# Two feature groups of the first projection side by side, turned blocks in 1 KB runs, and readers two ticks later

## The chip, the cores and the metric

The kernel runs on one core of a Trainium2 chip. The metric is device time in microseconds of one execution, the median of several. TensorE (PE) multiplies, VectorE (DVE) and ScalarE (ACT) do elementwise work, GpSimd (POOL) and SyncE (SP) here do little but issue transfers; ACT issues a few too.

## What is computed

Two decoder layers over 256 tokens of width 2048, float32 throughout. Layer 0 mixes with a gated spatial unit (A) and a gated recurrence (B), layer 1 with attention (C); each is followed by a gated feed-forward block with a causal convolution of width 3 over the tokens. Cut to what matters here:

```python
for l in range(DEPTH):                     # DEPTH = 2
    h = rms_norm(x, mix_norm[l])
    h = mixer_ab(h, ...) if l % 2 == 0 else mixer_c(h, ...)
    x = x + h
    h = rms_norm(x, ffn_norm[l])
    x = x + conv_ffn(h, ...)

def mixer_ab(h, w_in, ...):                # u, v, q, f, i, g = 6 x 1024 columns
    u, v, q, f, i, g = jnp.split(h @ w_in, cuts, axis=-1)
    v = rms_norm(gelu(v), v_gain)          # per head of 128
    y_a = gelu(u) * (causal(sp_w) @ v + sp_b)
    y_b = hgrn2(q, f, i, g, ...)
    return jnp.concatenate([y_a, y_b], axis=-1) @ w_out

def conv_ffn(h, w_up, conv_w, conv_b, w_down):
    z = h @ w_up                           # 2 x 5632 columns
    z = sum(conv_w[j] * zp[:, j:j + seq] for j in range(3)) + conv_b
    a, b = jnp.split(z, 2, axis=-1)
    return (silu(a) * b) @ w_down
```

## The kernel before

**Layout.** The residual stream `xT` lies feature-major: 16 tiles of 128 features by 256 tokens. A float32 product is made of three passes over operands split into a high and a low part (float32r): high by high, high by low, low by high. `weights` (L157) takes one tile of weights (128 x 1024, 512 KB): SP loads `w`, ACT copies it to `wh` (L176), DVE subtracts to get `wl` (L179). There are four `w` and three `wh` and `wl` buffers, and in the FFN two more of each for every other tile. Activations are split likewise by `split` (L279), into `a[k]`, 512 columns: high, then low; `Norm.feed_split` makes them from `xT[k]` and the norm's gain, `feed_square` adds up the squares, `finish` and `finish_tok` sum them over the partitions on PE (L360, L349) and take the reciprocal root.

**Projections.** `project_tok` and `project_four` make a token-major result of 512 features, two banks `ps[0]`, `ps[1]` of 128 tokens each, from eight tiles of weights (chunks of two k), twelve matmuls of 512 columns a chunk. `project` makes one head of 128 features, feature-major, from two tiles. PSUM has four `pm` banks for these and four `px` banks for small products.

**Ticks.** Each projection calls `tick()` once before each of its weight tiles. A tick advances up to `depth` generators of the `queue`, in which the elementwise work that follows a projection is written: one `yield` is one tick. `LAG = 4` is the number of ticks that a reader leaves after a turned block was sent off. The program's order is a wish: a compile-time scheduler draws the final order of every engine's instructions from it and from a model of when operands are ready, and each engine then runs its own list in order.

**Turned blocks.** `transposed` (L254) turns a token-major result of 128 x 1024 to feature-major: DVE transposes 32 x 32 blocks into `tmp` (L257, two instructions), then 16 transfers of 32 KB, SBUF to SBUF, alternately from SP and POOL, move block (a, b) to its place (L262). A transfer reads 32 partitions of 1 KB and writes four runs of 256 B in each. The result has four feature tiles of 256 tokens, each tile in one run. Readers: the residual adds in `add_four` (L385, after both `w_out`) and `add_y` (L911, after `w_down`), which then feed the next norm; the convolution `conv` in the FFN (L865 on ACT, L866 and L867 on DVE); `attend` for q and k (L713); `gate` for the attention output (L811, L812).

**First projection.** `project_tok(w_v[g], norm, feed=g == 0)` (L420) runs group 0 of v's columns and then group 1. While it runs group 0, x arrives: SP loads x pieces and weights in an order fixed by hand (`in_turn`, first nine weight tiles). The first eight k are loaded in halves of 256 KB (`SMALL = 8`, `single`). Group 1 uses the `a[k]` made for group 0. The squares of the norm are summed during group 1 by the generator `finish` (L410), three k a tick; the squares may not start before the seventh tile's `wh` (`deep["hold"]`), and ACT's six late loads of constants (L435) hang on the same. `finish` ends with the first group's Gelu; `drain()` runs what is left of it. After the stage come the norm of v per head (L452 to L463), the eight f heads (`project_norm(w_f[h])`) and, from the fourth tick on, the products `mix` (L470).

**FFN.** `up(j0)` projects four tiles of the first half (`za`), starts `gate`, then four of the second half (`zb`), and starts `fill`; both wait for the norm, turn their block with `empty` (L846), let LAG ticks go, and do one feature tile a tick. `room` gives one `tmp` and two `zt` buffers; the convolution has six rotating buffers. `down` multiplies hidden tiles as they come (`STEPS`); the last step has eight hidden tiles, so a quarter of the output takes four chunks, and each quarter goes through `add_y`.

Of the kernel before, what the change touches and what calls it, by code (L numbers as in the profile page):

```python
# [8 lines left out]
F32 = mybir.dt.float32  # L9
# [3 lines left out]
ALU = mybir.AluOpType  # L13
# [12 lines left out]
LAG = 4  # L26
# [5 lines left out]
SMALL = 8  # L32
# [19 lines left out]
def tile_trunk(ctx: ExitStack, tc: tile.TileContext, x, pp_d, cst_d, mlev_d, msk_d,  # L52
# [91 lines left out]
    def in_turn(r):  # L144
        if deep["turn"] > 9:
            return
        if deep["dma"] is not None:
            tc.add_manual_dep(r.ins, deep["dma"].ins.name, order, reason="queue order")
        deep["dma"] = r
# [7 lines left out]
    def weights(src, n, rows=None, single=None):  # L157
# [8 lines left out]
        parts = [slice(i, i + n // 2) for i in (0, n // 2)] if single else [slice(0, n)]  # L166
        for i, p in enumerate(parts):
            if single:
                fetch_x(single[1] + i)
            in_turn(nc.sync.dma_start(  # L170
                w[:, p] if rows is None else w.rearrange("p (m c) -> p m c", m=rows), src[:, p] if single else src))
        for i, p in enumerate(parts):
            if single:
                norm, k = single
                norm.feed_split(k + i, SC if k + i else V)
            deep["act"] = SC.activation(wh[:, p], w[:, p], AF.Copy)  # L176
            if deep["turn"] == 7:
                deep["hold"] = deep["act"]
            V.tensor_tensor(wl[:, p], w[:, p], wh[:, p].bitcast(F32), ALU.subtract)  # L179
        return wh, wl  # L180

# [26 lines left out]
    def project_tok(wsrc, norm, feed=False):  # L208
        ps = [pm.tile([P, 512], F32, tag="pm", name=nm("pm")) for _ in range(2)]
        k = 0  # L210
        for c in (2,) * 8:
            if feed and k >= SMALL:
                fetch_x(k)
                for i in range(c):
                    norm.feed_split(k + i)
            tick()
            wh, wl = weights(wsrc[:, k * 512:(k + c) * 512], c * 512, single=(norm, k) if feed and k < SMALL else None)
            if feed and k < SMALL:
                for i in range(c):
                    a = norm.a[k + i]  # L220
                    for j, (o, t) in enumerate(((0, wh), (S, wh), (0, wl))):
                        for T in range(2):
                            PE.matmul(ps[T], a[:, o + T * P:o + (T + 1) * P], t[:, i * 512:(i + 1) * 512],
                                      start=k + i + j == 0, stop=False)
                k += c
                continue
            for T in range(2):
                for i in range(c):
# [6 lines left out]
            k += c  # L235
# [18 lines left out]
    def transposed(src, tmp, dst, queues=(nc.sync, nc.gpsimd)):  # L254
# [5 lines left out]
        for a in range(4):  # L260
            for b in range(4):
                queues[(a + b) % len(queues)].dma_start(dst[BLK * b:BLK * (b + 1), :, a * n:(a + 1) * n],  # L262
                                  tmp[BLK * a:BLK * (a + 1), b * 4 * n:(b + 1) * 4 * n]
                                  .rearrange("p (m r) -> p m r", m=4))
# [110 lines left out]
    def add_four(q, ps, z, tmp, dst, nxt):  # L375
# [4 lines left out]
        def rest():  # L380
            for _ in range(LAG - (q == 3)):
                yield
            for i in range(4):
                m = 4 * q + i
                V.tensor_tensor(xT[m], xT[m], dst[:, i], ALU.add)  # L385
# [11 lines left out]
    def mixer_ab(norm):  # L397
# [12 lines left out]
        def finish():  # L410
            for k in range(KT):
                norm.feed_square(k)
                if k % 3 == 2:
                    yield
# [5 lines left out]
        for g in range(2):  # L420
            ps = project_tok(w_v[g], norm, feed=g == 0)
            v = hp.tile([P, 2, 512], F32, tag="tok", name=nm("gv"), bufs=2)
            gv.append(v)
            if g == 0:
                SC.activation(v[:, 0], ps[0], AF.Copy)
                SC.activation(v[:, 1], ps[1], AF.Copy)
                queue.append(finish())
# [229 lines left out]
        for q in range(4):  # L657
# [3 lines left out]
            dst = stage[:, q % 2].rearrange("p h c -> p (h c)").rearrange("p (m t) -> p m t", m=4)  # L661
# [399 lines left out]
```

## Time and profile before

| what | value |
|---|---|
| median of 3 runs | 2309.99 us (2309.86 to 2310.22) |
| the profiled execution | 2308.94 us |
| its span | 2306.8 us |
| granted PE clock | 1.0 |
| busy DVE, ACT, POOL | 68%, 56%, 14% |
| HBM read | 435.24 MB, 190 GB/s over the span |
| DMA packets under 512 B | 106400 of 462243 |
| first projection | 4.87 to 51.45 us |
| mixer C starts | 1112.4 us |

A line of the timeline gives start and duration in us, engine, line of the kernel, operation, the tile written and those read, the shape and how many were merged; in brackets, how long the engine had been idle and what ended that. A line of waits gives the waiting engine and line, what it waited for, the total in us, how often, and the longest. A line on one tile or source line gives the least, median and greatest duration in ns. A window's line gives its length, busy us and instruction count of PE, PE's weight loads, DVE, ACT and POOL, then the granted clock, the DMA engines' busy share and GB/s.

### The profile page before, as it was taken

The page shows a single profiled execution, that of the slowest core. Times are in us where ns is not written, and L with a number is a line of the kernel's source. Part 1 is how long each engine was busy: PE and PEld are TensorE (multiplying, and loading weights), DVE is VectorE, ACT ScalarE, POOL GpSimd, SP SyncE. Part 2 cuts the span into 40 slices and gives each one's busy share as a digit, 9 for nine tenths or more (in the row PEclk, how much of TensorE's full clock was granted, in tenths as well). Part 3 has the DMA queues.
Part 4 walks back from the last instruction along what each step waited for, and adds up shares of the span by engine and source line. Part 5 has one row for each costly group of instructions (what it writes and reads, how often), then busy time and mean ns, then how long its engine had stood idle before and what let it go on. Part 6 is the DMA issues. An engine that isn't in the chain of part 4 may idle for free. (4 is left out here: it accounts for less than half of the span.)

```text
span 2306.8 us, 31666 instructions
## 1 busy us (share of the span) xinstructions
PE 2298.1 (100%) x10608; PEld 1915.4 (83%) x10608; DVE 1575.4 (68%) x2407; ACT 1301.9 (56%) x1972; POOL 311.8 (14%) x579
## 2 busy tenths in 40 slices
PE   9999999999999999999999999999999999999999
PEld 7888888888888888888888888888888888888887
DVE  7778876776557656765866666666776476667666
ACT  7655665665555545654555555655665465455643
POOL 0000002122012002111111101121221022012102
PEclk9999999999999999999999999999999999999999
DMA  8655567877667767776666565777777677667765
GB/s 276 182 167 154 155 195 215 253 222 211 210 208 209 220 196 215 217 217 192 190 229 201 182 192 168 224 220 241 234 219 208 202 215 213 206 204 218 221 202 174
DMA packets 462243, 477.25 MB, mean 207 GB/s; under 512 B 106400, under 2 KB 424880, under 8 KB 461952
## 3 DMA queue, kind: packets, MB, share of 16 engines
q1 hardware_dynamic: 441840, 451.96, 63.6%
q0 software_dynamic: 18512, 20.93, 4.0%
q10 hardware_dynamic: 1728, 2.35, 0.3%
q8 instruction: 83, 1.36, 0.3%
q14 instruction: 80, 0.66, 0.1%
HBM read 435.24 MB, written 2.11 MB: 190 GB/s over the span
## 5 line engine op out<-in xcount | busy, mean ns | idle before, releaser
L179 DVE TENSOR_TENSOR wl<-w,wh 128x1024 fp32r<-128x1024 f32 (+1 forms) x822 | 997.9, 1218 | 637.9 <-ACT wh L176 627.4
L176 ACT ACTIVATE wh<-w 128x1024 fp32r<-128x1024 f32 (+1 forms) x822 | 863.8, 1054 | 798.7 <-PE pm L251 537.3
L249 PE MATMUL pm<-wh,a 128*128 128x512 f32 x1536 | 598.5, 390 | 0.0
L250 PE MATMUL pm<-wl,a 128*128 128x512 f32 x1536 | 597.7, 389 | 0.6 <-DVE wl L179 0.6
L251 PE MATMUL pm<-wh,a 128*128 128x512 f32 x1536 | 597.6, 389 | 0.0
L262 POOL DMA_DIRECT2D zt<-tmp x413 | 223.7, 549 | 1203.9 <-DVE tmp L257 1048.8
L250 PEld LDWEIGHTS pm<-wl,a 128*128 128x128 f32 x1536 | 288.3, 188 | 60.7 <-DVE wl L179 1.0
L251 PEld LDWEIGHTS pm<-wh,a 128*128 128x128 f32 x1536 | 288.3, 188 | 60.0
L249 PEld LDWEIGHTS pm<-wh,a 128*128 128x128 f32 x1536 | 288.3, 188 | 59.7
L250 PE MATMUL pm<-wl,hid 128*128 128x512 f32 x688 | 267.8, 389 | 0.2 <-DVE wl L179 0.2
L249 PE MATMUL pm<-wh,hid 128*128 128x512 f32 x688 | 267.6, 389 | 0.0
L251 PE MATMUL pm<-wh,hid 128*128 128x512 f32 x688 | 267.6, 389 | 0.0
L232 PE MATMUL pm<-wh,a 128*128 128x512 f32 x496 | 196.2, 396 | 0.0
L233 PE MATMUL pm<-wl,a 128*128 128x512 f32 x496 | 193.4, 390 | 0.8 <-DVE wl L179 0.8
L234 PE MATMUL pm<-wh,a 128*128 128x512 f32 x496 | 193.3, 390 | 0.0
L200 PE MATMUL pm<-a,wh 128*128 128x512 f32 x528 | 169.5, 400 | 0.0
L250 PEld LDWEIGHTS pm<-wl,hid 128*128 128x128 f32 x688 | 129.1, 188 | 27.3 <-DVE wl L179 0.6
L249 PEld LDWEIGHTS pm<-wh,hid 128*128 128x128 f32 x688 | 129.1, 188 | 26.9
L251 PEld LDWEIGHTS pm<-wh,hid 128*128 128x128 f32 x688 | 129.1, 188 | 26.8
L262 POOL DMA_DIRECT2D turn<-tmp x128 | 69.4, 550 | 392.4 <-DVE tmp L257 180.9
L203 PEld LDWEIGHTS pm<-a,wl 128*128 128x128 f32 x528 | 99.1, 188 | 22.8
L233 PEld LDWEIGHTS pm<-wl,a 128*128 128x128 f32 x496 | 93.2, 188 | 19.8 <-DVE wl L179 1.2
(218 smaller groups left out, 2227.7 us busy)
## 6 DMA issues: line engine op xcount, KB each, us to landing
w<-in_w_up SPq DMA_DIRECT2D x352, 512.0 KB, 4.6
w<-in_w_dn SPq DMA_DIRECT2D x176, 512.0 KB, 4.6
w<-in_w_cqkv SPq DMA_DIRECT2D x96, 512.0 KB, 4.4
w<-in_w_abo SPq DMA_DIRECT2D x32, 512.0 KB, 4.5
w<-in_w_cg SPq DMA_DIRECT2D x32, 512.0 KB, 4.5
w<-in_w_co SPq DMA_DIRECT2D x32, 512.0 KB, 4.7
zt<-tmp SPq DMA_DIRECT2D x414, 32.0 KB, 2.8
zt<-tmp POOLq DMA_DIRECT2D x413, 32.0 KB, 2.6
```

Of the source, the lines that this page charges most:

```text
L176: deep["act"] = SC.activation(wh[:, p], w[:, p], AF.Copy)
L179: V.tensor_tensor(wl[:, p], w[:, p], wh[:, p].bitcast(F32), ALU.subtract)
L200: PE.matmul(ps, wh[:, k * P:(k + 1) * P], acts[done + k], start=done + k == 0, stop=False, skip_group_check=True)
L203: PE.matmul(ps[:, S:2 * S], wl[:, k * P:(k + 1) * P], acts[done + k][:, 0:S], start=False, stop=done + k == nk - 1, skip_group_check=True)
L232: PE.matmul(ps[T], ah, h, start=k + i == 0, stop=False)
L233: PE.matmul(ps[T], ah, l, start=False, stop=False)
L234: PE.matmul(ps[T], al, h, start=False, stop=k + i == KT - 1)
L249: PE.matmul(ps[T], ah, h, start=k + i == 0, stop=False)
L250: PE.matmul(ps[T], ah, l, start=False, stop=False)
L251: deep['mm'] = PE.matmul(ps[T], al, h, start=False, stop=k + i == n - 1)
L262: queues[(a + b) % len(queues)].dma_start(dst[BLK * b:BLK * (b + 1), :, a * n:(a + 1) * n], tmp[BLK * a:BLK * (a + 1), b * 4 * n:(b + 1) * ...
```

## The change

`LAG` goes from 4 to 6 and `SMALL` from 8 to 4. Four things change.

The first projection is a function of its own, `project_first`, a generator that gives the banks of group 0 and then of group 1. It holds all four `pm` banks. For the first eight k both groups' weights are loaded and used for each pair of k; for the last eight, group 0 comes first, then group 1. The very first load is weights, then x. The squares may start behind the ninth tile of weights, where `then` puts `finish` in the queue; `finish` yields after every second k. All of the stage's loads are now in the order fixed by hand.

`transposed` writes each block into one run of 1 KB per partition, so that tile m of the result lies in four runs of 64 tokens, 256 elements apart (`block`). `natural=True`, for the attention output alone, keeps the old form. All other readers use such views.

The convolution's six buffers are fixed tiles of 256 + 64 columns, the last 64 cleared once per FFN; its two multiply-adds run over all 256 columns, the shifted ones into the extra columns.

Readers of turned blocks leave six ticks, four in the last quarter (three before), and three for the last FFN's third quarter as before; `gate` in mixer C keeps its six and four.

```diff
-LAG = 4
+LAG = 6
-SMALL = 8
+SMALL = 4
...
+    def project_first(wsrc, norm, then):
+        ps = [[pm.tile([P, 512], F32, tag="pm", name=nm("pm")) for _ in range(2)] for _ in range(2)]
...
+        for k in range(0, KT // 2, 2):
+            w3 = [three(1024) for _ in range(2)]
+            if k < SMALL:
+                for i in range(2):
+                    cols = slice(i * 512, (i + 1) * 512)
+                    for g in range(2):
+                        if g == 1 or k + i:
+                            fetch_x(k + i) if g == 0 else None
+                        in_turn(nc.sync.dma_start(w3[g][0][:, cols], wsrc[g][:, (k + i) * 512:(k + i + 1) * 512]))
+                        if g == 0 and k + i == 0:
+                            fetch_x(0)
+                for i in range(2):
+                    cols = slice(i * 512, (i + 1) * 512)
+                    for g in range(2):
+                        if g == 0:
+                            norm.feed_split(k + i, SC if k + i else V)
+                        halves(*(t[:, cols] for t in w3[g]))
...
+                continue
+            fetch_x(k)
+            for i in range(2):
+                norm.feed_split(k + i)
+            for g in range(2):
+                in_turn(nc.sync.dma_start(w3[g][0], wsrc[g][:, k * 512:(k + 2) * 512]))
+                halves(*w3[g])
+            for g in range(2):
+                for T in range(2):
+                    piece(k, 2, g, *w3[g][1:], range(2), T)
+        for g in range(2):
+            for k in range(KT // 2, KT, 2):
...
+                if "hold" in deep:
+                    tick()
+                w, wh, wl = three(1024)
+                in_turn(nc.sync.dma_start(w, wsrc[g][:, k * 512:(k + 2) * 512]))
+                r = halves(w, wh, wl)
+                if "hold" not in deep:
+                    deep["hold"] = r
+                    then()
+                for T in range(2):
+                    piece(k, 2, g, wh, wl, range(2), T)
+            yield ps[g]
...
-                queues[(a + b) % len(queues)].dma_start(dst[BLK * b:BLK * (b + 1), :, a * n:(a + 1) * n],
-                                  tmp[BLK * a:BLK * (a + 1), b * 4 * n:(b + 1) * 4 * n]
-                                  .rearrange("p (m r) -> p m r", m=4))
+                d, t = dst[BLK * b:BLK * (b + 1)], tmp[BLK * a:BLK * (a + 1), b * 4 * n:(b + 1) * 4 * n]
+                if natural:
+                    d = d.rearrange("p (m t) -> p m t", m=4)[:, :, a * n:(a + 1) * n]
+                    t = t.rearrange("p (m r) -> p m r", m=4)
+                else:
+                    d = d[:, a * 4 * n:(a + 1) * 4 * n]
+                queues[(a + b) % len(queues)].dma_start(d, t)
+
+    def block(t, i):
+        return t.rearrange("p (a m r) -> p m a r", a=4, m=4)[:, i]
+
+    def four_by(t):
+        return t.rearrange("p (a r) -> p a r", a=4)
...
-            for _ in range(LAG - (q == 3)):
+            for _ in range(LAG - 2 * (q == 3)):
                 yield
...
-                V.tensor_tensor(xT[m], xT[m], dst[:, i], ALU.add)
+                V.tensor_tensor(four_by(xT[m]), four_by(xT[m]), block(dst, i), ALU.add)
...
-                if k % 3 == 2:
+                if k % 2:
                     yield
...
-        for g in range(2):
-            ps = project_tok(w_v[g], norm, feed=g == 0)
+        for g, ps in enumerate(project_first(w_v, norm, lambda: queue.append(finish()))):
...
-                SC.activation(qk[:, j].rearrange("p (t n) -> p t n", t=2), turned(t[:, h % 4]), AF.Copy, scale=g)
+                SC.activation(qk[:, j].rearrange("p (t a i) -> p t a i", t=2, a=4),
+                              view(t, (h % 4) * 2 * BLK, (1, 2), (8 * BLK, 4), (2, BLK)), AF.Copy, scale=g)
...
-            for _ in range(LAG + 2 * (q < 3)):
+            for _ in range(LAG - 2 * (q == 3)):
                 yield
...
+        convs = [hp.tile([P, S + LANE], F32, tag=f"conv{i}", name=f"conv{i}") for i in range(6)]
+        for c in convs:
+            V.memset(c[:, S:], 0.0)
...
-            c = hp.tile([P, S], F32, tag="conv", name=nm("conv"), bufs=6)
-            SC.activation(c, z, AF.Identity, bias=pp[:, cb:cb + 1], scale=w(2))
-            V.scalar_tensor_tensor(c[:, 1:], z[:, :S - 1], w(1), c[:, 1:], ALU.mult, ALU.add)
-            V.scalar_tensor_tensor(c[:, 2:], z[:, :S - 2], w(0), c[:, 2:], ALU.mult, ALU.add)
-            return c
+            c = convs[turns[0] % 6]
+            turns[0] += 1
+            SC.activation(four_by(c[:, 0:S]), z, AF.Identity, bias=pp[:, cb:cb + 1], scale=w(2))
+            for i in range(2):
+                t = four_by(c[:, i + 1:S + i + 1])
+                V.scalar_tensor_tensor(t, z, w(1 - i), t, ALU.mult, ALU.add)
+            return c[:, 0:S]
...
-                for _ in range(LAG - (near or q == 3)):
+                for _ in range(3 if near else LAG - 2 * (q == 3)):
                     yield
```

## The prediction

> **What bounds the kernel now.** I read the page's busy shares first, then the list of what PE waited for, then PE's timeline where a wait is named, then DVE, ACT, SP and POOL around those places.
>
> ```profile
> PE 2298.1 (100%) x10608; PEld 1915.4 (83%) x10608; DVE 1575.4 (68%) x2407; ACT 1301.9 (56%) x1972; POOL 311.8 (14%) x579
> PEclk9999999999999999999999999999999999999999
> ```
>
> PE is busy for 2298.1 of 2306.8 us at the full granted clock. A matmul of 512 columns starts every 0.227 us wherever its operands are ready (17.90, 18.35, 18.58 and so on in the timeline below), so busy PE is here PE at its pace. The change removes no matmul. What it can win is PE's waits:
>
> ```profile
> PE pm L223 <- ACT wh L176: 1.9, 3, 1.1
> PE warm L136 <- DVE one L84: 1.1, 1, 1.1
> PE pm L250 <- DVE wl L179: 0.8, 2, 0.6
> PE pm L233 <- DVE wl L179: 0.8, 1, 0.8
> PE px L470 <- DVE gv L463: 0.6, 1, 0.6
> ```
>
> Without the warm-up's 1.1 that is 4.1 us in eight places. By matmul starts (distance less 0.227) the places are: 0.83 before the first projection matmul at 4.87, then 0.45 at 6.81, 1.28 at 9.61, 0.77 at 61.72, 0.96 at 1119.0, 0.77 at 1493.9, 0.35 at 2215.7: 5.4 us, 0.23% of the run. That is the ceiling of any gain.
>
> ```profile
> 4.87 1.20 PE L223 MATMUL pm<-wh,a 128*128 128x512 f32 x4 [0.46 <-ACT wh L176]
> ...
> 6.81 1.21 PE L223 MATMUL pm<-wh,a 128*128 128x512 f32 x4 [0.28 <-ACT wh L176]
> ...
> 9.61 1.19 PE L223 MATMUL pm<-wh,a 128*128 128x512 f32 x4 [1.12 <-ACT wh L176]
> ...
> 42.38 0.59 PE L360 MATMUL px<-acc,ones 128*128 128x256 f32 x2
> ...
> 51.45 0.62 PE L200 MATMUL pm<-a,wh 128*128 128x512 f32 x2
> ...
> 61.72 0.49 PE L470 MATMUL px<-wt,gv 128*128 128x128 f32 x2 [0.60 <-DVE gv L463]
> ```
>
> These lines give the first stage: three waits for loads, the norm's sum (L360) 9.1 us before the projection ends at 51.45, and mixer A's first matmul (L470) waiting for `gv`.
>
> **Part 1, the start.** Now a feature piece k needs 128 KB of x and 256 KB of weights for six matmuls, 6 x 0.227 = 1.36 us: 282 KB/us. Side by side it needs 640 KB for twelve, 2.72 us: 235 KB/us. Counts of loads are the same (8 of 256 KB, 12 of 512 KB, 9 of x), all still on SP's queue.
>
> ```profile
> 0.00:10.00 10.00, 7.08 (x28) 5.51 (x29) 4.09 (x10) 4.82 (x8) 0.20 (x4) 1.00 0.70 215
> 10.00:20.00 10.00, 10.00 (x46) 8.26 (x45) 9.06 (x17) 9.03 (x18) 0.00 (x0) 1.00 1.05 405
> ```
>
> The last column says that loads run at 215 GB/s in the first 10 us and at 405 after, so only the first pieces starve. First matmul: today ACT starts on the first weights at 4.19, and 0.68 us later PE starts. The weights now go ahead of x, so x lands last, about then, and needs only DVE's 0.35 (L295): 4.19 + 0.35 + 0.06 = 4.6, a gain of 0.27. After that, 384 KB are usable at 4.19, 768 at 6.13 and 1024 at 8.13 (ACT's starts): 162 to 198 KB/us. The new k = 1 needs 1024 KB, usable at 7.4 to 8.1, plus 0.63 for `wh`: 8.0 to 8.8, against 4.6 + 2.72 = 7.3. PE is then 0.7 to 1.4 late, and the faster loads after 10 us leave no more. Today it is 9.61 - (4.87 + 2.72) = 2.0 late. I take 1.1: gain 0.27 + 0.9 = **1.2 us** (bounds: a gain of 1.6; a loss of 0.5 if the second group's 256 KB delay each next x by 256/162 = 1.6 us, less what PE has to do meanwhile).
>
> **Part 2, the norm's sum moves to the end of the stage.** Its 16 squares (ACT, 0.40 each) and 15 adds (DVE, 0.42) start behind the ninth tile of weights instead of the seventh and go two a tick. Seven ticks and a drain follow: L360, L349, the reciprocal root, the table load and the first two Gelus now stand behind the last projection matmul. ACT's six late loads of constants hang on the same tile; they move from 19.7 to about 21 us, well ahead of use. PE loses nothing by L360 itself. But from L360 (42.38) to `gv` ready for L470 (61.7) is a chain of 19.3 us on ACT and DVE. It now starts at 4.6 + 1.1 + 192 x 0.227 = 49.3, and ends at 68.6 if nothing shortens it. PE's work between 51.45 and L470 was 9.5 us, so an L470 left in its place would be reached at 49.3 + 0.8 + 9.5 = 59.6. Nothing in PE's queue can pass it. In the trace L470 stands amid a head's matmuls, between an L200 and an L203 and not at a chunk's start where the program puts it, so the order was drawn by expected readiness; I expect it later in the queue, with a wait like today's. DVE is busy 23.3 of 25 us from 50 to 75 already, and it also feeds `wl`, so a cost is as likely as a gain: **0**, bounds -0.8 (today's wait gone) and +9.0.
>
> **Part 3, 1 KB runs.** Each turned block is 16 transfers of 32 KB, half issued by SP, half by POOL:
>
> ```profile
> L262 SPq DMA_DIRECT2D zt<-tmp x414: 585/599/1815, 426.3 to 2297.4; - x138
> L262 POOL DMA_DIRECT2D zt<-tmp x413: 548/548/565, 426.6 to 2296.6; - x138
> ```
>
> SP's loads with one run per partition take 0.33 to 0.43 to issue, so eight fall by about 8 x 0.2 = 1.6 us; I take this row, the nearest, though a floor of no saving is possible. Packet records: SP's transfers are 128 packets of 256 B at 19.6 ns each, 157 ns over 16 engines; as 32 of 1024 B at 52 ns, 104 ns. POOL's are 16 packets of 2 KB today, so its half need not change, and a block is done when both halves are. PE has no wait for these transfers but 2215.7's. **0 on the path.** The Trainium skill ("DMA: Bandwidth & Descriptors", section "Why small descriptors are slow (HBM only)") says that SBUF to SBUF transfers don't suffer from small descriptors. By that rule this part frees nothing; the packet records speak mildly against it; the sum is 0 by both.
>
> **Part 4, strided readers.** Four runs of 64 elements for 256 in one:
>
> ```profile
> L812 DVE TENSOR_TENSOR yc<-turn,yc x16: 598/614/635, 1441.8 to 1511.5; 128x256 fp32r<-128x256 f32 x16
> L911 DVE TENSOR_TENSOR x<-x,zt x32: 377/417/425, 1092.9 to 2302.1; 128x256 f32<-128x256 f32 x32
> L283 ACT ACTIVATE a<-x,pp x32: 506/512/532, 339.6 to 1598.7; 128x256 fp32r<-128x256 f32 x32
> ```
>
> A read that steps four elements costs 0.2 us more on DVE (614 against 417); one that steps two costs little (512, against 495 for L293 without steps). The new views run through 64 neighbours, so I take 0. At the 0.2 bound, 352 conv passes add 70 us to DVE's 1575 over 1.4 ms, still under PE. The Trainium skill ("SBUF — State Buffer", the note on cachelines in section "Door 1: The DMA port swizzle") lets accesses that share a 16-byte line pass at full rate and charges each crossing; the four-element row above agrees, and the new runs are free by it too. The six halo memsets per FFN are 0.06 to 0.17 each (L84, L83), beside PE's first chunks: 0; uncovered, 1 us.
>
> **Part 5, two ticks later.** A tick is one chunk, 2.72 us. In the FFN a half-step has 16 ticks and its readers end at tick 10 instead of 8, so `zt` (two buffers) comes free in time, and `hid` is a whole step ahead. DVE and ACT stop waiting for turned blocks, which ended in the 0.35 at 2215.7: **-0.35**. The gate loop before `w_co` keeps its six and four ticks and its old layout, so 1493.9 stays. The tight place is FFN 0's last step, where a quarter is only 4 ticks. Behind its handover to mixer C (1112.4) stand 10 feeds instead of 8 (two of quarter 1, four each of 2 and 3), 0.42 + 0.48 + 0.42 = 1.3 us of DVE each. SP's transfers for quarter 2 also wait for quarter 0's last add, two ticks on, with the weight loads queued behind them; DVE runs about three chunks ahead of PE, which covers two ticks (5.4 us if not). Weight splits now precede the feeds that made PE wait at 1119, so that 0.96 can go, while 2.6 us of feeds come later before `a[12]` is used at chunk 7. Bounds -0.96 and +2.6; I take **-0.4**. At the end of the kernel, quarter 1's last two adds are drained behind the last matmul's add in the program. DVE idles 2.7 us before 2298.1, which takes them in; if not, two adds and an issue, 1.2 us. **0.**
>
> **Sum.** -1.2 + 0 - 0.35 - 0.4 = -1.95 us. Profiled, 2308.94 becomes 2307.0 (span 2306.8 to 2304.9). The median shown is 2309.99, 1.05 above that execution, and becomes **2308.0 us**.
>
> **Rivals.**
> *Given back.* The new order wins 1.2 at the start and pays it at `gv` or the handover by a wait of 1 to 3 us: 2309 to 2311.5, say 2310.3. For it: DVE is over 87% busy in both places (39.4 of 45 us in 1085 to 1130). Against: PE's lead of some 5 us hid most of such crowding so far.
> *Slower: L470 blocks PE.* If the compiled order keeps L470 where it is relative to the heads, PE waits 68.6 - 59.6 = 9.0 us in one piece, and today's 0.77 goes: 2309.99 - 1.95 - 0.77 + 9.0 = 2316.3. It decides once PE reaches L470 over 6.6 us ahead of `gv` (4.6 beyond the 1.95 won). Against it: the drawn order follows readiness.
> *Faster by over 0.2%.* All seven waits but the first go: 5.4 - 0.8 + 0.27 = 4.9: 2305.1. It needs 1493.9 too, which the change doesn't touch.
> *Not what it says.* POOL's half is in long packets already; if it lands last, blocks arrive as before, and only the later reading helps: 2308.0 all the same.
>
> **How the numbers follow.** Forecast 0.56 (the last rival is within it), given back 0.22, L470 or the handover blocking PE by over 6 us 0.15, all waits gone 0.07. About 0.2% (4.6 us) is what a measurement of this kernel can tell from no change, so the first two cases are "same", 0.78; slower 0.15; faster 0.07. The range goes from 2305.6 (start -1.6, 61.7 -0.8, 1119 -0.96, 2215.7 -0.35, and 0.7 of 1493.9) to 2313.5 (handover +2.6 and 2.1 at `gv` with nothing won beyond the start): the L470 case lies outside.
>
> **What would show it.** First projection matmul near 4.6 with weights first; one wait of about 1 us before 10 us in place of two; the stage's last matmul near 49.3, L360 behind it; L470 later than 61.7, with a wait under 1 us; no wait near 1119 and 2215.7; SP's `zt` issues near 0.4 us, packets under 512 B down from 106400 to near 37000 (73472 of SP less the 4096 of the gate blocks that keep their form); DVE conv still 0.48. A wait at L470, or at the seventh chunk of mixer C, of more than 3 us would make the forecast wrong, and so would any lower granted clock.

## The result: 0.5% slower, outside the forecast range

The changed kernel takes 2320.8 us (median of 5 runs, 2318.8 to 2322.06); the kernel before, beside it, 2309.99 (5 runs, 2309.23 to 2310.22). The ratio is 1.0048, 95% interval 1.0033 to 1.0062: slower by more than the 0.2% that the prediction took for measurable, where 2308.0 and "same" were forecast. The profiled execution took 2322.04 us, its span is 2320.3 (before 2308.94 and 2306.8).

In the new file the weight conversions `wh` and `wl` are L167 and L168, the matmuls of a chunk L292 to L294 (mixer C's projections L276 to L278), the transposes L301, the transfers L312, the convs L927 and L930, the x additions L974, the z evictions L910. First the busy shares and the granted clock, from the page:

```profile
PE 2303.7 (99%) x10608; PEld 1917.1 (83%) x10608; DVE 1578.8 (68%) x2419; ACT 1300.6 (56%) x1972; POOL 283.2 (12%) x579
PEclk9999999999999999999999999999999999999999
```

Then what PE waited for (us in all, times, longest):

```profile
PE pm L293 <- DVE wl L168: 4.2, 5, 1.3
PE pm L276 <- ACT wh L167: 2.5, 1, 2.5
PE pm L277 <- DVE wl L168: 1.5, 3, 0.8
PE warm L136 <- DVE one L84: 1.1, 1, 1.1
PE pm L278 <- DVE a L351: 0.7, 1, 0.7
PE pm L258 <- ACT wh L167: 0.5, 1, 0.5
```

PE does the same matmuls, and waits for converted weights in places where it had waited for nothing. L276's 2.5 us is one wait, which ends at 1184 us. By matmul starts (distance less 0.2268 us for 512 columns, where it is more), summed over stages of each profiled execution, and with the time from the last matmul to the end of the span below them:

| us lost by PE in | before | after | e4, no 1 KB runs | e9, old transfers in the new order | e15, new transfers, readers held |
|---|---|---|---|---|---|
| 0 to 400 | 29.4 | 27.7 | 27.5 | 27.9 | 27.5 |
| 400 to 1100, feed-forward 0 | 0.9 | 2.1 | 0.9 | 5.2 | 1.3 |
| 1100 to 1150, handover to mixer C | 1.6 | 3.4 | 0.6 | 0.6 | 3.6 |
| 1150 to 1200, mixer C's q and k | 2.4 | 7.9 | 2.5 | 1.8 | 7.1 |
| 1200 to 1500 | 14.1 | 14.1 | 14.6 | 14.6 | 14.1 |
| 1500 to the last matmul | 1.8 | 5.9 | 2.4 | 5.2 | 1.7 |
| behind the last matmul | 3.6 | 6.1 | 3.5 | 3.5 | 3.4 |
| span | 2306.8 | 2320.3 | 2305.1 | 2311.8 | 2312.0 |

After less before, row by row: -1.7 + 1.2 + 1.8 + 5.5 + 0 + 4.1 + 2.5 = 13.4 of the 13.5 us by which the span grew. The first row is the start's gain; all others are losses. The last three columns are experiments, told below.

The start did what was forecast in the trace. PE's timeline of the changed kernel:

```profile
4.52 1.93 PE L209 MATMUL pm<-wh,a 128*128 128x512 f32 x4
...
48.96 0.59 PE L415 MATMUL px<-acc,ones 128*128 128x256 f32 x2
```

The first projection matmul is at 4.52 and the norm's sum at 48.96. The 1 KB form didn't make the transfers quicker. Issues of one block's pieces, with minimum, median and longest ns of one, on SP and on POOL:

```profile
L312 SPq DMA_DIRECT2D zt<-tmp x414: 507/588/1627, 424.6 to 2311.4; - x138
...
L312 POOL DMA_DIRECT2D zt<-tmp x413: 496/496/498, 424.9 to 2310.5; - x138
```

SP's median issue went from 599 to 588 ns and POOL's from 548 to 496. From issue to landing the page gives 2.7 us on SP's queue (2.8 before) and 2.6 on POOL's (2.6). Packets under 512 B did fall, from 106400 to 36384. The Trainium skill's rule that was weighed in Part 3 ("DMA: Bandwidth & Descriptors", "Why small descriptors are slow (HBM only)") stands: between SBUF and SBUF the longer runs freed nothing that matters here.

**Where the loss begins.** ACT's waits name it. First of the kernel before, then of the changed one:

```profile
ACT conv L865 <- DMA zt<-tmp: 16.7, 12, 3.8
ACT conv L927 <- DMA zt<-tmp: 110.0, 43, 7.9
```

The convs waited 16.7 us in 12 places before, and 110.0 us in 43 now. One block on ACT, in the changed kernel, and under it the same block in e4, which is the change without its 1 KB form (columns: start, duration, engine, line, operation, out<-in, count; in brackets idle time before it and what ended it):

```profile
480.06 0.69 ACT L910 ACTIVATE z<-pm,Rt 128x512 f32<-128x512 f32 x1 [0.67 <-PE pm L294]
480.64 1.05 ACT L167 ACTIVATE wh<-w 128x1024 fp32r<-128x1024 f32 x1
482.77 1.06 ACT L167 ACTIVATE wh<-w 128x1024 fp32r<-128x1024 f32 x1 [1.08 <-PE pm L294]
485.49 1.06 ACT L167 ACTIVATE wh<-w 128x1024 fp32r<-128x1024 f32 x1 [1.66 <-PE pm L294]
489.44 1.09 ACT L927 ACTIVATE conv<-zt,pp 128x256 f32<-128x256 f32 x2 [2.89 <-DMA zt<-tmp]
490.44 1.04 ACT L167 ACTIVATE wh<-w 128x1024 fp32r<-128x1024 f32 x1
```

```profile
479.72 0.69 ACT L892 ACTIVATE z<-pm,Rt 128x512 f32<-128x512 f32 x1 [0.67 <-PE pm L294]
480.31 1.05 ACT L167 ACTIVATE wh<-w 128x1024 fp32r<-128x1024 f32 x1
482.44 1.06 ACT L167 ACTIVATE wh<-w 128x1024 fp32r<-128x1024 f32 x1 [1.08 <-PE pm L294]
485.16 1.06 ACT L167 ACTIVATE wh<-w 128x1024 fp32r<-128x1024 f32 x1 [1.66 <-DMA zt<-tmp]
487.88 1.06 ACT L167 ACTIVATE wh<-w 128x1024 fp32r<-128x1024 f32 x1 [1.66 <-PE pm L294]
489.11 1.09 ACT L906 ACTIVATE conv<-zt,pp 128x256 f32<-128x256 f32 x2 [0.17 <-issue]
```

In both the conv starts 8.7 us behind the end of its z eviction: the block lands when it lands. But in the changed kernel the conv stands behind the third conversion in ACT's order, and the fourth, which could have run at about 488.2, is stuck behind it until 490.44. In the trace of before all 44 blocks have four conversions between z eviction and conv; in the changed kernel all 44 have three. That place matters because of when the blocks land: the last piece lands 7.6 us (median of the 44) behind z's eviction, 7.8 before the change. ACT is through with the third conversion after 5.8 us and with the fourth after 8.5 (the block shown). So in the old order 12 of the 44 blocks land after ACT is ready for them (the 12 waits above), in the new one 43. One chunk of PE's lead over its weights is gone at every block. Mostly the rest covers it. Where a block lands late, it doesn't.

### The profile page after: what moved, and what is told of

It is laid out like the page before. It is cut to its first block, busy times and chain, and to the rows that moved or that the text cites. A ratio compares the mean times of both kernels' runs of the same rounds, so it can differ in the third digit from the quotient of the medians.

```text
span 2320.3 us, 31753 instructions
## 1 busy us (share of the span) xinstructions
PE 2303.7 (99%) x10608; PEld 1917.1 (83%) x10608; DVE 1578.8 (68%) x2419; ACT 1300.6 (56%) x1972; POOL 283.2 (12%) x579
## 5 line engine op out<-in xcount | busy, mean ns | idle before, releaser
L168 DVE TENSOR_TENSOR wl<-w,wh 128x1024 fp32r<-128x1024 f32 (+1 forms) x822 | 997.0, 1216 | 560.4 <-ACT wh L167 552.2
L167 ACT ACTIVATE wh<-w 128x1024 fp32r<-128x1024 f32 (+1 forms) x822 | 863.2, 1052 | 672.0 <-PE pm L294 449.3
L293 PE MATMUL pm<-wl,a 128*128 128x512 f32 x1536 | 598.2, 389 | 4.2 <-DVE wl L168 4.2
L292 PE MATMUL pm<-wh,a 128*128 128x512 f32 x1536 | 598.5, 390 | 0.0
L294 PE MATMUL pm<-wh,a 128*128 128x512 f32 x1536 | 597.6, 389 | 0.0
L312 POOL DMA_DIRECT2D zt<-tmp x413 | 201.8, 497 | 1236.0 <-DVE tmp L301 1086.5
L293 PEld LDWEIGHTS pm<-wl,a 128*128 128x128 f32 x1536 | 288.3, 188 | 66.0 <-DVE wl L168 6.5
L292 PEld LDWEIGHTS pm<-wh,a 128*128 128x128 f32 x1536 | 288.3, 188 | 59.8
L294 PEld LDWEIGHTS pm<-wh,a 128*128 128x128 f32 x1536 | 288.3, 188 | 59.8
L292 PE MATMUL pm<-wh,hid 128*128 128x512 f32 x688 | 267.6, 389 | 0.0
L294 PE MATMUL pm<-wh,hid 128*128 128x512 f32 x688 | 267.6, 389 | 0.0
L930 DVE SCALAR_TENSOR_TENSOR conv<-zt,pp,conv 128x256 f32<-128x256 f32 x352 | 158.9, 481 | 92.2 <-ACT conv L927 68.9
L276 PE MATMUL pm<-wh,a 128*128 128x512 f32 x448 | 178.8, 399 | 2.5 <-ACT wh L167 2.5
L277 PE MATMUL pm<-wl,a 128*128 128x512 f32 x448 | 176.2, 393 | 1.5 <-DVE wl L168 1.5
L278 PE MATMUL pm<-wh,a 128*128 128x512 f32 x448 | 175.7, 392 | 0.7 <-DVE a L351 0.7
L927 ACT ACTIVATE conv<-zt,pp 128x256 f32<-128x256 f32 x176 | 99.9, 591 | 117.4 <-DMA zt<-tmp 110.0
L292 PEld LDWEIGHTS pm<-wh,hid 128*128 128x128 f32 x688 | 129.1, 188 | 26.9
L294 PEld LDWEIGHTS pm<-wh,hid 128*128 128x128 f32 x688 | 129.1, 188 | 26.7
```

The lines of the kernel that those rows point to most:

```text
L167: r = SC.activation(wh, w, AF.Copy)
L168: V.tensor_tensor(wl, w, wh.bitcast(F32), ALU.subtract)
L276: PE.matmul(ps[T], ah, h, start=k + i == 0, stop=False)
L277: PE.matmul(ps[T], ah, l, start=False, stop=False)
L278: PE.matmul(ps[T], al, h, start=False, stop=k + i == KT - 1)
L292: PE.matmul(ps[T], ah, h, start=k + i == 0, stop=False)
```

## The experiments

Two theories at first. A: the 1 KB form moves the compiled place of the readers one chunk nearer to their transfers, and conversions queue behind waiting readers. B: the start does it, by the norm's sum that moved. A third, C: POOL has pauses of 2.2 to 2.9 us (below), and the change only shifts them to places where they hurt.

The runs were made in four groups, each with the kernel before beside it (2308.58, 2309.76, 2310.05 and 2309.18 us). Runs of different groups are therefore compared by their distance from the kernel before; the changed kernel stands 10.8 us above it.

**e1 to e4, the parts.** e1 takes the new first stage into the kernel before; e2 takes the 1 KB form with its views; e3 takes six ticks; e4 is the change less the 1 KB form. Their diffs are the hunks shown above.

> Only the first projection with both groups side by side; the turned pieces' form and the readers' distance are as before. Theory A (1 KB form moves the compiled readers one chunk earlier, ACT's and VectorE's order then waits for the pieces): about 2308.5 us, the start's gain of 1.2 to 1.7 us kept whole, last z eviction to first conv about 8.4 us with 4 weight conversions between, tail 3.6 us. Theory B (the start, by the norm's sum moved): slower than before by a good part of the 10.8 us. Theory C (POOL's pauses fall elsewhere because fewer instructions stand ahead of them): anything from 2308 to 2313, by where the pauses fall.

> Only the 1 KB form of the transfers, with the readers' strided views; distance 4 (6 at the attention's output) and the first projection as before. Theory A: about 2320 us (the 11 us loss, and the start's gain not there), 3 weight conversions between the z eviction and the first conv, the tail 2 to 3 us longer, ACT's conv waiting for zt in about 40 places. Theory B: 2310. Theory C: PE waits only behind POOL's pauses, and the tail as before.

> Only the readers' distance of six ticks instead of four, in the old 64-run form. Theory A: 2309 to 2311, since the compiled order keeps 4 weight conversions ahead of the first conv. A rival, that six ticks pile the readers up at the stages' ends (handover of the first feed-forward to mixer C, 2.2 us of waits after the change): 2312 or more, with the waits at about 1118 to 1131 us there.

> The change without its 1 KB form: first projection side by side and six ticks, pieces in 64 runs of 256 B pairs as before. Theory A: 2308 to 2309, tail 3.6 us. Were the distance of six ticks the cause, 2315 or more; were it the first projection, the same.

| | median us (runs) | before beside it | ratio, 95% interval | conversions from z to conv |
|---|---|---|---|---|
| e1 start only | 2308.04 (10) | 2308.58 | 0.9994 [0.9985, 1.0003] | 4 in 44 of 44 |
| e2 runs only | 2326.06 (4) | 2308.58 | 1.0074 [1.0059, 1.0089] | 3 in 44 of 44 |
| e3 lag only | 2308.96 (10) | 2308.58 | 1.0002 [0.9992, 1.0011] | 4 in 44 of 44 |
| e4 no runs | 2307.45 (10) | 2308.58 | 0.9997 [0.9987, 1.0006] | 4 in 44 of 44 |

B falls: with the 1 KB form the loss is there, and without it nothing is measurably lost. But e2 loses 17.5 us, more than the whole change and more than the 2320 us expected, so the parts don't add: with the new form, the start and the two ticks together take some 7 us off. The start's gain (span 2305.4 for 2306.8) isn't resolved by e1's medians. In e2 ACT's wait for `zt` is 102.7 us, in e4 18.6. The ticks don't place the readers: in the new form the conv stands behind the third conversion with four ticks (e2) as with six (the changed kernel), in the old form behind the fourth with either (e1, e3, e4).

**e5, the readers held back.** The convs are asked for at nine ticks and pinned behind the latest conversion, and the x additions behind the next transposes:

```diff
-                for _ in range(LAG):
+                for _ in range(9):
...
+            tc.add_manual_dep(r.ins, deep["wh"].ins.name, order, reason="not before")
+            deep["conv"] = r
...
+                    tc.add_manual_dep(r.ins, deep["T"].ins.name, order, reason="not before")
```

and the next conversion is pinned behind `deep["conv"]`.

> The changed kernel whole, with one thing added: in the feed-forwards the first conv of a block is pinned behind the fourth weight conversion after the z eviction on ACT (38 of 44 blocks; the changed kernel has the third), and the x additions behind the next quarter's transposes, as both stood before the change. The attention's readers and the handover to mixer C are left alone. Theory A (the readers' place in the order): PE's waits at 758, 1642, 1654 and 2090 us (0.94, 1.1, 0.8, 1.5) and the 2.5 us of the tail go: 2320.8 less 6.8, about 2314; the 4.05 us at 1184 and about 2.2 at 1118 to 1131 stay. Rival (POOL's pauses alone, wherever the readers stand): only the tail goes, 2318. Rival (the 1 KB transfers themselves cost, by ports or by the strided reads): 2319 or more.

Measured: 2315.78 us, ratio 1.0027 [1.0017, 1.0036], 6.0 above the kernel before: 4.8 less than the changed kernel, against 6.8 expected. ACT's wait for `zt` falls from 110.0 to 43.2 us. The waits at 758, 1642, 1654 and 2090 us are gone, the tail is 3.4 us. But 2.2 us appear at 1127.8, where a sum of the norm (L408) waits for DVE. C alone doesn't explain the loss: the pauses stand where they stood.

**e6, the other way round, missed.** Old transfers, with the next conversion pinned behind a conv emitted at eight ticks.

> The other way round: side-by-side start and six ticks with the old 64-run transfers (the kernel that took 2307.45), but the first conv of a block pinned ahead of the fourth weight conversion, so that 3 stand between it and the z eviction (42 of 44 blocks). The transfers, the reads and the x additions are the old ones. Theory A: ACT waits for zt at its convs 80 us or more in all (18.6 before), PE waits about 1 to 2 us behind each of POOL's pauses that lies in a feed-forward (about 700, 1480, 1760 us), 2310 to 2314, tail as it was. If the 1 KB form itself is the cause: 2307.5, as without the pin.

Measured: 2306.7 us, ratio 0.9987 [0.9977, 0.9996]. Three conversions now stand between z and conv, yet the median time from z's end to the conv is 8.48 us, as good as e4's 8.44 (changed kernel: 7.86, from 7.07 up), since one conversion more had moved ahead of z. The readers weren't nearer, ACT waits 11.2 us for `zt`, and the run says nothing on A, except that the count of conversions between z and conv isn't what costs by itself. It is the one kernel here whose interval lies below 1.

**e9, the same with ACT's new sequence.** e6 mended: the conv is emitted at six ticks and the second conversion emitted after it is pinned behind it.

```diff
+        if deep.get("conv") is not None:
+            deep["skip"] += 1
+            if deep["skip"] > 1:
+                tc.add_manual_dep(r.ins, deep["conv"].ins.name, order, reason="not before")
+                deep["conv"] = None
```

> The pin of e6 moved did not bring the convs nearer in time, so once more: old 64-run transfers and old x additions, side-by-side start and six ticks, with one weight conversion pinned behind each block's first conv so that ACT's compiled order in the feed-forwards is that of the changed kernel (z, z, three conversions, two convs, a conversion, a conv ...; 33 of 36 blocks alike). Theory A (the readers' place): ACT's conv waits for zt about 100 us in all, and PE about 1 us behind each POOL pause in a feed-forward (700, 1480, 1762, 2194 us): 2310 to 2312, tail as before. Theory D (the 1 KB form itself): 2307.5 and 10 to 20 us of conv waits.

Measured: 2314.81 us (10 runs), ratio 1.0020 [1.0011, 1.0030], 4.8 above the kernel before. e4, which it equals but for the order, stands 1.1 below. ACT's waits for `zt`, in e4 and in e9:

```profile
ACT conv L906 <- DMA zt<-tmp: 18.6, 10, 4.5
ACT conv L911 <- DMA zt<-tmp: 90.3, 39, 6.6
```

D, that the 1 KB form itself costs, falls as the whole cause: with the old 64 runs the order alone costs 5.9 us (6.7 by the spans), about half of the 12 that lie between e4 and the changed kernel. By the table it costs at least as much in the feed-forwards as the change did, and nothing at the handover and the k block. The same block in e4 and in e9 shows how. POOL, at the same pause (e9):

```profile
699.63 0.55 POOL L310 DMA_DIRECT2D zt<-tmp  x1 [17.42 <-DVE tmp L305]
702.68 3.81 POOL L310 DMA_DIRECT2D zt<-tmp  x7 [2.50 <-issue]
```

ACT in e4, then in e9:

```profile
702.76 1.06 ACT L167 ACTIVATE wh<-w 128x1024 fp32r<-128x1024 f32 x1 [1.66 <-PE pm L294]
705.48 1.06 ACT L167 ACTIVATE wh<-w 128x1024 fp32r<-128x1024 f32 x1 [1.66 <-PE pm L294]
711.05 2.08 ACT L906 ACTIVATE conv<-zt,pp 128x256 f32<-128x256 f32 x4 [4.51 <-DMA zt<-tmp]
```

```profile
703.33 1.06 ACT L167 ACTIVATE wh<-w 128x1024 fp32r<-128x1024 f32 x1 [1.61 <-PE pm L299]
712.82 1.10 ACT L911 ACTIVATE conv<-zt,pp 128x256 f32<-128x256 f32 x2 [8.42 <-DMA w<-in_w_up]
713.82 1.04 ACT L167 ACTIVATE wh<-w 128x1024 fp32r<-128x1024 f32 x1
```

POOL stops for 2.50 us inside the block in both. In e4 ACT has converted once more (705.48) and then waits 4.51; PE loses nothing. In e9 the conv comes first, ACT sits for 8.42 us, and PE loses 4.1 us in 700 to 750. (The bracket names a weight load, as the last to land by the profile. The conv reads `zt`, whose last piece from POOL landed at 711.99.)

**e7, e10, e11, e13, POOL's pauses.** e7 adds 24 memsets on POOL at the start, e10 40 small transfers; e11 and e13 add 77 and 95 such transfers to e4:

```diff
+    for _ in range(40):
+        nc.gpsimd.dma_start(idle[0:BLK], pp_d[0:BLK, 0:16])
```

> The changed kernel with 24 more instructions on POOL at the very start (memsets of unused padding), as many as three blocks' transfers. If POOL's pauses come by the count of its instructions, they come three blocks earlier, and the 4.05 us wait at 1184 us, behind the pause in the attention's q block, goes or moves: 2315 to 2318, other waits of 1 to 2 us behind the pauses' new places, tail still 6 us. If the pauses come by something else (time, packets, bytes), 2320.8 with the same waits.

> The changed kernel with 40 small transfers more on POOL at the start, where it is idle. POOL's pauses so far come after transfers 113, 219, 326, 432 and 538 in the old form and 128, 249, 370 and 491 in the new, whatever else POOL does. If transfers are what counts, the pauses move 40 transfers earlier, out of the attention's q block, and PE's wait at 1184 us with its 6 us at half clock goes: about 5 us less, 2315 to 2317, with waits of about 1 us behind the other pauses. If the pauses do not move: 2320.8.

> The old transfers (side-by-side start, six ticks, 2307.45 us) with 77 small transfers more on POOL at the start, so that its third pause falls behind transfer 249, in the attention's q block, as in the changed kernel. If the pause's place alone decides: PE waits about 4 us at 1184 us and the clock drops, 2312 to 2313. If it needs the readers nearer as well: under 1 us there, 2307 to 2309.

> As e11, with 95 small transfers in place of 77: its pauses then came behind old transfers 51, 157, 264, 370 and 476, and moved by 62 for 77 extra, so 18 more should bring the third to 249 to 252, inside the attention's q block at about 1165 us. If the pause's place alone decides: PE waits about 4 us at 1178 us and its clock halves for some us, 2312 to 2314. If the changed kernel's readers must stand nearer as well: under 1 us there, 2307 to 2309.

In the changed kernel the pause behind transfer 249 falls into the pieces of k in mixer C (the expectations call it the q block; the reader L766 takes the gain of k there). POOL, ACT, and then windows (busy us of PE, PEld, DVE, ACT, POOL with counts; granted clock; DMA share; GB/s):

```profile
1169.50 0.50 POOL L312 DMA_DIRECT2D turn<-tmp  x1 [8.73 <-DVE tmp L301]
1172.87 3.43 POOL L312 DMA_DIRECT2D turn<-tmp  x7 [2.87 <-issue]
```

```profile
1173.73 1.05 ACT L167 ACTIVATE wh<-w 128x1024 fp32r<-128x1024 f32 x1
1182.22 0.93 ACT L766 ACTIVATE qk<-turn,pp 128x256 f32<-128x256 f32 x2 [7.44 <-DMA w<-in_w_cqkv]
1183.06 2.93 ACT L167 ACTIVATE wh<-w 128x1024 fp32r<-128x1024 f32 x3
```

```profile
1180.00:1184.00 4.00, 1.66 (x8) 1.04 (x6) 0.00 (x0) 1.78 (x3) 0.56 (x1) 0.96 0.72 261
1184.00:1190.00 6.00, 5.39 (x12) 3.92 (x13) 3.50 (x3) 1.99 (x3) 0.00 (x0) 0.50 0.94 382
```

The reader of k's pieces stops ACT for 7.44 us (a weight load is named, as the last to land by the profile); three conversions are stuck behind it; PE stops for 2.49 us at 1181.7, and then runs at half the clock for 6 us. That makes the 5.5 us of the stage.

e7 measured 2322.73 us, ratio 1.0057 [1.0042, 1.0072], with every pause behind the same transfer as without the memsets: they come by transfers. e10 measured 2327.37, 1.0073 [1.0058, 1.0088], 6.5 more than the changed kernel by their distances instead of 5 less. The pauses did move by 40 transfers and the loss in 1150 to 1200 went (7.9 to 2.4), but those at the new places cost as much: 7.5 us in 1100 to 1150, 4.0 in 1500 to 1550 at a clock of 0.61 in 1526 to 1530, and with a pause at 2313 the tail is 8.8. e11 measured 2309.61, 0.9996 [0.9986, 1.0005]; its pause came 15 transfers past the block it was meant for, and another cost 1.9 us at 1976. e13 measured 2310.14, 1.0008 [0.9999, 1.0018]; its pause hit the q block, the one ahead of k's (POOL of e13):

```profile
1160.36 2.71 POOL L308 DMA_DIRECT2D turn<-tmp  x5 [35.49 <-DMA w<-in_w_cqkv]
1165.30 1.63 POOL L308 DMA_DIRECT2D turn<-tmp  x3 [2.22 <-issue]
```

PE then waited 0.57 and 1.03 us and the clock stayed at 1.00; the stage lost 3.2 us against e4's 2.5. Two others of its pauses cost 4.1 us (at 445) and 1.5 (at 792) in the profiled execution, which with 2314.20 us is one of the three long ones of ten.

So C is half right. The changed kernel loses behind all four of its pauses: 0.94 us at 758, the k block, 1.1 and 0.8 at 1642 and 1654, 1.5 at 2091. The old order (e4) loses nothing behind its pauses at 699, 1093 and 1761, 1.4 us behind that at 1478 and 1.0 behind that at 2177. It isn't immune, but by the medians moving the pauses costs it 2.1 us at most (e4 1.1 below the kernel before, e11 0.4 below, e13 1.0 above), and the three intervals overlap.

**e8, e14, the tail.** e8 holds the x additions behind the next quarter's transposes in both feed-forwards, e14 in the last one only (`if last:`).

> The changed kernel, with the x additions alone held behind the next quarter's transposes, as they stood before the change. Theory A: the tail returns from 6.1 to about 3.6 us and nothing else moves: 2318.3. If the tail is long because the 1 KB transfers land later there, it stays 6 us: 2320.8.

> The changed kernel with the x additions held behind the next quarter's transposes in the last feed-forward only. If the additions' place makes the tail: tail 3.3 to 3.6 us instead of 6.1, PE as in the changed kernel, 2318.3. If e8's 2.8 us more of PE waits came from there: 2320.8 or more.

The end on DVE, changed kernel, then e14:

```profile
2303.67 1.10 DVE L974 TENSOR_TENSOR x<-x,zt 128x256 f32<-128x256 f32 x3 [3.61 <-DMA zt<-tmp]
2304.68 1.22 DVE L168 TENSOR_TENSOR wl<-w,wh 128x1024 fp32r<-128x1024 f32 x1
2305.82 1.28 DVE L1018 TENSOR_TENSOR y<-y,pm 128x512 f32<-128x512 f32 x2
2307.01 1.30 DVE L301 STREAM_TRANSPOSE tmp<-y 128x512 f32<-128x512 f32 x2
```

```profile
2301.46 1.28 DVE L1020 TENSOR_TENSOR y<-y,pm 128x512 f32<-128x512 f32 x2
2302.75 1.31 DVE L301 STREAM_TRANSPOSE tmp<-y 128x512 f32<-128x512 f32 x2
2303.97 2.06 DVE L974 TENSOR_TENSOR x<-x,zt 128x256 f32<-128x256 f32 x6
```

In the changed kernel DVE waits 3.61 us for pieces that it needs last, ahead of the sum and transposes that the third quarter's transfers wait for. In e14 these go first, and the tail is 3.5 us instead of 6.1. The median is 2319.69, ratio 1.0047 [1.0035, 1.0060], 10.5 above the kernel before and so 0.3 less than the changed kernel, where 2.5 were expected: the tail is shown in the trace, not resolved by the medians. e8, with 2321.26 and 1.0050 [1.0035, 1.0065], has a tail of 3.5 us too, but its PE ends 2.8 us later, 1.7 of them at the handover, where the first feed-forward's additions were held as well.

**e12, e15, both remedies.** e12 is e5 with e10's transfers, e15 is e5 with the additions held in the last feed-forward only.

> Both remedies on the changed kernel: readers held back in the feed-forwards (2315.8 alone) and the pauses 40 transfers earlier. Theory A with the pause in the q block as a second cause: the two gains add up, 2315.8 less 5, about 2310.5, with the 2.2 us at the handover to mixer C left. If 1 KB transfers cost something further, 2313 or more.

> As e5 (convs pinned behind the fourth conversion), with the x additions held in the last feed-forward only. If e5's 2.5 us at 1128 us came from holding the first feed-forward's additions: 2313 to 2314.5, with the 5 us behind the pause at 1182 us left. If not: 2315.8.

e12 measured 2317.29, 1.0030 [1.0020, 1.0041]: 1.2 more than e5 by their distances, with intervals that overlap, and not 5 less. The pauses cost 4.6 us in 1500 to 1550 instead, and one at 2302 makes the tail 6.5 us. e15 measured 2314.29, 1.0024 [1.0015, 1.0033], 5.1 above the kernel before: 5.7 less than the changed kernel. ACT's wait in it:

```profile
ACT conv L931 <- DMA zt<-tmp: 47.8, 32, 5.8
```

Its column in the table is within 0.4 us of that of before in both feed-forwards and behind the last matmul, with the pauses where the changed kernel has them; what is left is the handover (3.6 against 1.6) and the k block (7.1 against 2.4).

## Why the prediction was wrong

**Part 1 was right.** 4.52 for 4.6, with 0.48 us of wait before it (0.83 before the change); then waits of 0.34 and 0.28 us by 6.1 in place of the one of 1.1; the waits of the first 50 us fell by 1.7 us for the 1.2 forecast. (The "eight places" of today's waits are seven; the sum is right.) **Part 2** too: the sum at 48.96 for 49.3; mixer A's first product comes later in the queue, at 66.69, and waits for nothing, while a head's projection at 62.07 waits 0.62 us for `wh`. The rival that it blocks PE didn't come. **Part 4** too: conv 481 ns on DVE (479 before) and 591 on ACT (589), x additions 418 (417).

**Part 3 is the step that failed: "0 on the path."** Its reasoning was that PE had no wait for these transfers but one of 0.35 us, and that a block is complete when both halves are. Both hold, and SP's issue time hardly fell (588 ns for 599, where about 400 was expected). But a change of the transfers' form also changed the drawn order of ACT and DVE, which the prediction treated as set by ticks. It had noticed that the order "was drawn by expected readiness", and had used it for L470 alone. With 1 KB runs the readers stand one chunk nearer, while the pieces land as late as before; e9 gives 5.9 us to this with the old transfers, and e15 takes 5.7 us away from the new ones. That is about half of the loss. The largest single place, the k block, is a second effect of the form that the prediction left out: POOL's pauses come every 121 transfers instead of 106, and one fell on the pieces of k. There the clock fell too, which the prediction had named as a sign of being wrong. Why the order is drawn so was not measured; that the 1 KB transfers are taken for quicker than they are fits all the kernels here, and is only argued. Nor was it separated which part of e2's edit moves the order, the transfers, the strided views or the fixed convolution buffers.

**Part 5 failed with it.** That the readers end "at tick 10 instead of 8" in effect didn't happen: on ACT they came nearer. The 0.35 at 2215.7 did go, and so did 1493.9's, but ACT and DVE wait more for turned blocks, not less (110.0 us for 16.7; DVE's x additions 14.2 for 0.5). The handover was put at -0.4, bounds -0.96 and +2.6: it measured +1.8, inside its bounds by luck: the bound was reckoned for two ticks more, and with these and the old transfers (e4) the row is 0.6. Lag alone (e3) is 1.0002. "At the end of the kernel ... 0" is +2.5 by the table, by DVE's order (e14's trace).

**The rivals.** None named this mechanism. The one on the slower side had the right form, an engine's order with a late operand ahead of what PE needs, but at L470. POOL's late half was named as a reason for no gain, not as a source of lateness.

**What stays open.** Whether the k block's pause would cost 5.5 us in the old order as well: e13 came nearest, one block off, with waits of 1.6 us. ACT is ready for k's reader 5.6 us behind the transposes in the changed kernel and 6.5 in e4, so by these times (an estimate) the nearer place is 0.9 of the reader's 7.44 us and the pause is most of it. The handover's 2 us weren't isolated. Held readers and moved pauses didn't add up (e12), because a moved pause lands in some other block.

## What to carry to other kernels

A change that only makes a transfer's form look cheaper can move its consumers in an order drawn by expected readiness; before costing such an edit at nothing, count what stands between producer and consumer on each in-order engine, and what is queued behind the consumer. Idle time on ACT or DVE is harmless only while nothing that the bounding engine needs stands behind it. A lag counted in program steps is no guarantee of distance: compare the positions in the trace, and the times too, since e6 has the changed kernel's count and loses nothing.

## What the runs showed of the hardware

POOL, which issues half of the transfers, stops for 2.2 to 2.9 us at a regular count of them: behind transfers 113, 219, 326, 432 and 538 in the old form (106 or 107 apart), 128, 249, 370 and 491 in the new (121 apart). 538, 128 and 370 stand at the end of a block; there it is the next block's first issue that comes some 3 us late (in the changed kernel 4.0 us behind z's eviction instead of 1.0). Memsets don't count (e7), small transfers do (e10). The last pieces of a block that is hit land up to 12.7 us behind its transposes in the changed kernel, where the median of all blocks is 6.9.

PE's clock fell to 0.50 after a single wait of 2.49 us at 1181.7 (512-column matmuls 0.427 us apart for some 6 us), which added 2.1 us to that wait's price. In e5 one of 2.2 us, at 1127.8, brought half clock for 3.4 us. Single waits of up to 1.5 us elsewhere in the changed kernel left it at 1.00, while in e9 two of 0.9 and 1.4 us close together, at 715, brought it to 0.76 over the 6 us from 718 (half clock for 3.4 us of it). The Trainium skill ("TensorE: Matmul & The Clock Gate", "Part 1: The HAM clock gate (the "warmup" mystery)") gives the two states, full and half, and an idle window of about 3.4 us as what leads from full to half. The halves agree; the waits that did it were shorter than that window.
